# The low part of the rotary query over 128 rows of the key tile instead of 64

## The chip, the core and the metric

The kernel runs on one core of a Trainium2 chip. The metric is device time in microseconds (us), the median of several runs. The engines are called PE (TensorE, matmuls), PEld (the loading of PE's weights), DVE (VectorE), ACT (ScalarE), POOL (GpSimd) and SP (SyncE, which here only issues DMAs).

## The reference, cut to what matters

Two layers (DEPTH = 2) of a decoder trunk over 2048 tokens of width 1024, in float32. Each layer mixes gated linear attention (4 heads) with softmax attention (4 heads), and adds the projected result to the residual. The part that the change touches is the score of the softmax attention:

```python
q = concat([q[..., :128], apply_rope(q[..., 128:], cos, sin)])   # 128 plain + 64 rotary
k = concat([k[..., :128], apply_rope(k[..., 128:], cos, sin)])
for each block of 128 queries, each head:
    s = einsum('bhqd,bhkd->bhqk', q_blk, k) * 192 ** -0.5
    s = where(key <= query, s, -inf)
    p = softmax(s)
    o = einsum('bhqk,bhkd->bhqd', p, v)
```

A score is a dot product over 192 numbers: 128 plain ones and 64 rotary ones.

## The kernel before

**Precision.** Matmul operands are of type fp32r. To keep the precision of float32, each operand is split into a high part (the value rounded to fp32r) and a low part (the rest), and a product a·b is made as three: high·high, high·low and low·high.

**Stages.** Each layer has a first pass over 16 tiles of 128 tokens (input projection, linear attention), a second pass (gates, and the queries of all heads), then the softmax attention (`phase_b`), then the output projection (`phase_c`). `phase_b` goes through 32 steps, one for each head h (4) and each group g of 256 queries (8).

**Scores.** In a step, `scores` takes two blocks of 128 queries. For each it goes over the keys in banks of up to 512 columns, and makes each bank with five matmuls into one PSUM tile `sp`: three over the plain part (L951 to L953: query high · key high, query high · key low, query low · key high), then two over the rotary part. For the rotary part the tile `kr` holds the high part of the 64 rotary rows of the key in its rows 0 to 63 and the low part in its rows 64 to 127. The query's tile `qrr` holds the high part twice (`qrr[:, 0]`, rows 0 to 63 and 64 to 127), so that L954 makes high · high and high · low in one matmul over 128 rows. What is left, query low · key high, is L955, a matmul over 64 rows: `qrr[0:64, 1]` against `kr[0:64]`.

```python
T.matmul(o, lhsT=qrr[:, 0, ts_], rhs=kr[:, c0:c1], start=False, stop=False)            # L954
T.matmul(o, lhsT=qrr[0:64, 1, ts_], rhs=kr[0:64, c0:c1], start=False, stop=True)       # L955
```

DVE takes each bank out of PSUM (L959 with the mask on the diagonal, L962 elsewhere) and keeps the row maxima; ACT makes the exponentials (L969). There are two PSUM tiles `sp`.

**Values.** `values` of the step before runs interleaved with `scores` of the present one. For each 256 keys, PE transposes four 128x128 pieces of the probabilities into a tile `tp` (L88, of which there are three), ACT and DVE split it into the high part `ph` (L1004) and the low part `pl` (L1005), and PE multiplies with the values (L1024 to L1026). POOL scales the gates by the reciprocal of the softmax sum (L983, tile `gt`).

**Keys and queries.** `Gens` makes a step's keys, values and queries ahead of its scores: `lat` (loads), `kv` (projection; POOL writes the rotary key into `gst`, L869), `t` (transposes; ACT and DVE write the plain query `qn`, L886 and L887) and `tr` (rotary part; ACT and DVE write `kr` and `qrr`). A tile `q` holds `qn` and `qrr` of a step. There are four of them in `phase_b`; the queries of the first steps of a layer are made in the second pass, in tiles of their own.

**What sets the order.** On PE the order is that of the program, which interleaves scores, values and generation by estimated times (PACE, `pump`). On ACT, DVE, POOL and the DMA queues a scheduler sets it at build time. Every engine runs its instructions in its fixed order and waits for semaphores.

Of the kernel before, what the change touches and what calls it, by code (L numbers as in the profile page):

```python
# [9 lines left out]
F32 = mybir.dt.float32  # L10
# [9 lines left out]
P = 128  # L20
# [12 lines left out]
NSTG = 3  # L33
# pair of tiles and block of the second pass beside which a tile's queries are made; the pair that takes in the
# keys and values of each of the first head's first groups
QPOS = [(0, 3), (1, 1), (1, 3), (2, 1), (2, 3), (3, 0)] + [(p, b) for p in range(3, 7) for b in (1, 3)] + [(7, 0), (7, 1)]
PRE = (2, 4, 5, 6)
# pacing of phase B, per layer: lead of the generation of keys and queries over the attention (offset, ratio),
# lead of a step's scores over the step before's values (and in the last step), transposes ahead in the last step
PACE = [(-1.0, 0.151, 5.4, 2.1, 2, 10),  # L40
# [10 lines left out]
def trunk(ctx: ExitStack, tc: tile.TileContext, x, positions, norm_g, w_in, w_up, b_up, gla_g,  # L51
# [77 lines left out]

# [1 line left out]
    pos_f = cos.rearrange("p t c -> p (t c)")[0:NT, 0:P]  # L131

    def rotary(pool, ps):
        tr(ps[:, 0:NT], pos_f)
        pos = pool.tile([P, NT], F32, name="pos", bufs=1)
        V.tensor_copy(pos, ps[:, 0:NT])
        ang = pool.tile([P, NT, 32], F32, tag="osn", name="ang")
        V.tensor_tensor(out=ang, in0=pos.unsqueeze(2).broadcast_to([P, NT, 32]),
                        in1=cst[:, C_IF:C_IF + 32].unsqueeze(1).broadcast_to([P, NT, 32]), op=ALU.mult)
        kk = pool.tile([P, NT, 32], F32, tag="osn", name="kk")  # L140
        magic = 1.5 * 2.0 ** 23
        V.tensor_scalar(out=kk, in0=ang, scalar1=float(np.float32(1.0 / (2 * math.pi))), scalar2=magic,
                        op0=ALU.mult, op1=ALU.add)
        V.tensor_scalar(out=kk, in0=kk, scalar1=-magic, scalar2=None, op0=ALU.add)
        rest = 2 * math.pi
        for i in range(5):
            if i < 4:
                e = math.floor(math.log2(rest)) - 7
                c = math.floor(rest / 2.0 ** e) * 2.0 ** e
            else:  # L150
                c = float(np.float32(rest))
            V.scalar_tensor_tensor(out=ang, in0=kk, scalar=-c, in1=ang, op0=ALU.mult, op1=ALU.add)
            rest -= c
        lim = 3.1415925
        V.tensor_scalar(out=ang, in0=ang, scalar1=lim, scalar2=-lim, op0=ALU.min, op1=ALU.max)
        # cos(a) = sin(pi/2 - |a|)
        V.tensor_scalar(out=kk, in0=ang, scalar1=-1.0, scalar2=None, op0=ALU.mult)
        V.tensor_tensor(out=kk, in0=ang, in1=kk, op=ALU.max)
        V.tensor_scalar(out=kk, in0=kk, scalar1=-1.0, scalar2=math.pi / 2, op0=ALU.mult, op1=ALU.add)
        A.activation(out=cos, in_=kk, func=AF.Sin)  # L160
        tc.keep_in_program_order(A.activation(out=sin, in_=ang, func=AF.Sin))
        tc.keep_in_program_order(A.preload_act_table_set("natural_log_exp_and_others"))
        V.tensor_scalar(out=nsin, in0=sin, scalar1=-1.0, scalar2=None, op0=ALU.mult)

    def rope(eng, pool, o, i, n, c, s, ns, tag, u=None):
        # o, i: [P, n, 64]; c, s, ns: [P, n, 32]
        if u is None:
            u = pool.tile([P, n, 64], F32, tag=tag, name="ropeu", bufs=1)
        c2 = c.unsqueeze(2).broadcast_to([P, n, 2, 32])
        eng.tensor_tensor(out=u.rearrange("p n (a b) -> p n a b", a=2),  # L170
                          in0=i.rearrange("p n (a b) -> p n a b", a=2), in1=c2, op=ALU.mult)
        w = pool.tile([P, n, 64], F32, tag=tag + "w", name="ropew", bufs=1)
        eng.tensor_tensor(out=w[:, :, 0:32], in0=i[:, :, 32:64], in1=ns, op=ALU.mult)
        eng.tensor_tensor(out=w[:, :, 32:64], in0=i[:, :, 0:32], in1=s, op=ALU.mult)
        eng.tensor_tensor(out=o, in0=u, in1=w, op=ALU.add)

# [1 line left out]
    def layer_g8(l):  # L178
# [4 lines left out]
    def layer_small(l):  # L183
# [17 lines left out]
        sdma(r["gkr"], k_g[l, P:192].partition_broadcast(P))  # L201
        # against the high, low and high parts of the factor: high, high and low parts of the weights
        w3 = lp.tile([96, 256], F32, name="w3", bufs=1)
# [21 lines left out]

# [1 line left out]
    def wchunk(stage, kk, src, cols, n, name, scale, lo=None, us=None, halves=(0, 1)):  # L227
        """src: [1024, *] in DRAM, cols: (first here, first there, width); stage: gives a [P, >=kk, n] tile
        of which kk row blocks are filled at a time; scale: ("rows", g8) or ("gla", g)."""
        us, pieces = wpieces(stage, kk, src, cols, n, name, scale, lo, us, halves)  # L230
        for load, split in pieces:
            load()
            split()
        return us
# [53 lines left out]
    wi, wo = {}, {}  # L288
    # column groups of the input projection: c_q | c_kv | k_pe | the gate's low-rank factor; q | k; v; gates
    COLS = {"mi": ([(0, 1552, 448), (448, 1024, 16)], 464), "qk": ([(0, 0, 512)], 512),  # L290
# [16 lines left out]
    def boot_stage(which):  # L307
        # the first chunks are staged in units that nothing else uses yet
        got = {}

        def stage(half, k0):
            if half not in got:
                got[half] = unit([P, 4, COLS[which][1]], F32, f"boot{which}{half}")
            return got[half][:, k0:k0 + 2, :]

        return stage
# [24 lines left out]

    # ================= phase A, first pass: q, k, v, latents, rotary key; GLA =================
    def pass1(l, wp, pp, w1):
        sm = smalls[l]
        # the gate's low-rank factor as high | low | high parts (with a one for the bias), 32 columns each
        lr = w1.tile([P, 2, 3, 32], F32R, name="lr", bufs=1)
# [11 lines left out]
        def prep_r(t, n=2):  # L358
            # n tiles at a time
            if l == 0:  # L360
# [87 lines left out]
        def gla_b(t, qk):  # L448
# [6 lines left out]
            if t > 0:  # L455
# [8 lines left out]
                V.tensor_tensor(out=Tr[:, 1], in0=Tt, in1=Tr[:, 0].bitcast(F32), op=ALU.subtract)  # L464
            # high and low parts of the keys and (transposed, later) the queries
            kq = wp.tile([P, 4, 256], F32R, tag="stg", name="kq", bufs=3)
# [95 lines left out]
        def pair(p):  # L562
# [20 lines left out]
            if not more:  # L583
                # the second pass's weights, a piece at a time
                for which, blks in (("gt", (2, 3)), ("mg", (4, 5))):
# [24 lines left out]
        if l > 0:  # L610
            # stages that the end of the layer before takes in
            prep_x(0)
            yield
            prep_r(0, 1)
            yield
            prep_t(0, 0)
            yield
            prep_t(0, 1, True)
            yield
# [45 lines left out]

    # ================= phase A, second pass: output gates; keys and queries of the first head =================
    class pass2:
# [144 lines left out]

    # ================= keys, values and queries of 256 tokens of a head =================
    class Gens:
# [57 lines left out]
        def t(self, h, g):  # L872
# [5 lines left out]
            for i in range(2):  # L878
# [5 lines left out]
                                   in1=kn[:, 0, lt].bitcast(F32), op0=ALU.mult, op1=ALU.subtract)  # L884
            qn, qrr = self.aq(h, g)
            A.activation(out=qn[:, 0, :], in_=ps[:, 1, :], func=AF.Copy)  # L886
            V.tensor_tensor(out=qn[:, 1, :], in0=ps[:, 1, :], in1=qn[:, 0, :].bitcast(F32), op=ALU.subtract)  # L887
# [17 lines left out]

    # ================= phase B: attention, one head after the other =================
    def phase_b(l, pre):
        sm = smalls[l]
        goff, gratio, slead, slast, vlead, ypos = PACE[l]
        with tc.tile_pool(name=f"bp{l}", bufs=2, reuse_waits="tile") as bpl, \  # L910
# [15 lines left out]
            def scores(h, g):  # L926
# [6 lines left out]
                for i in range(2):  # L933
# [3 lines left out]
                    pt = both[:, i, :] if g < NG // 2 else unit([P, S], F32, f"p{l}")  # L937
                    # the last two of 512 + 128 keys become 320 + 320 where no boundary of a half lies between
                    edges = list(range(0, n, 512)) + [n]
# [5 lines left out]
                    for b in range(nbank):  # L945
# [8 lines left out]
                        T.matmul(o, lhsT=qrr[:, 0, ts_], rhs=kr[:, c0:c1], start=False, stop=False)  # L954
                        T.matmul(o, lhsT=qrr[0:64, 1, ts_], rhs=kr[0:64, c0:c1], start=False, stop=True)  # L955
                        w = c1 - c0
# [184 lines left out]

    # ================= phase C: output projection and residual =================
    def phase_c(l, wp, pp, yT01, ahead):
# [121 lines left out]
```

## Time and profile before

| | us |
|---|---|
| median of 3 runs | 2412.43 (2408.6 to 2414.42) |
| span of the profiled execution | 2413.8 |
| PE busy | 2364.2 (98% of the span) |
| PE weight loads (PEld) | 1938.4 (80%) |
| DVE busy | 1454.8 (60%) |
| ACT busy | 1315.5 (54%) |
| POOL busy | 411.8 (17%) |
| chain of work that ended last, PE's share | 90% |

The profiled execution's span is 1.4 us above the median; no other time of that execution is given, so the span stands for it. A matmul's row gives its start and its modelled duration. Matmuls are pipelined: the next one can start before the one before has ended, so that what a matmul costs in a dense stretch is read from the distance between starts, not from durations. The granted clock of PE in the profile is a mean between its two levels of 1.2 and 2.4 GHz, as a share of the higher.

### The profile page before, as it was taken

To read this page: it belongs to the slowest core of one execution; us is meant where nothing else is said; L and a number is where in the kernel's file an instruction comes from. 1 tells how busy PE (TensorE), PEld (TensorE's weight loads), DVE (VectorE), ACT (ScalarE), POOL (GpSimd) and SP (SyncE) were. 2 spreads that over 40 slices of the span, in tenths; PEclk is the share of its full clock that TensorE was granted. 3 is DMA by queue.
4 is the path that set the end of the run, shared out by engine and by line. 5 is a ranking of instruction groups with operands and counts; after the bars stand their busy time and mean duration, and the time that the engine had idled before them with its cause. 6 is when DMAs were issued, how large, how long until landed. Compare 5 with 4: busy or idle time off the path is not lost.

```text
span 2413.8 us, 37411 instructions
## 1 busy us (share of the span) xinstructions
PE 2364.2 (98%) x12821; PEld 1938.4 (80%) x12821; DVE 1454.8 (60%) x4376; ACT 1315.5 (54%) x3622; POOL 411.8 (17%) x593
## 2 busy tenths in 40 slices
PE   7999999999999999999999999999999999999999
PEld 5888888888787877788878888888887777777887
DVE  6676566666778777633365555656658777776222
ACT  6455456667766666532244444567666666665110
POOL 2111102333111112110011011033321111122000
PEclk9999999999999999999999999999999999999999
DMA  5111124432201111155531111344331111112542
GB/s 163 66 66 50 70 83 151 132 128 95 75 27 49 32 35 48 43 160 158 180 118 66 45 66 66 117 133 136 117 108 45 39 34 37 32 50 66 175 153 83
DMA packets 175859, 210.97 MB, mean 87 GB/s; under 512 B 17315, under 2 KB 128534, under 8 KB 175670
## 3 DMA queue, kind: packets, MB, share of 16 engines
q1 hardware_dynamic: 175254, 208.48, 26.8%
q8 instruction: 101, 1.65, 0.3%
q14 instruction: 88, 0.72, 0.1%
q0 software_dynamic: 416, 0.12, 0.1%
HBM read 128.86 MB, written 79.69 MB: 86 GB/s over the span
## 4 chain that ended last, share of the span: by engine, by line
PE 90%; ACT 4%; DVE 4%; DMA 1%; issue 1%; POOL 0%; SPq 0%; DVEq 0%; ACTq 0%
PE tp L88 10%; PE sp L955 5%; PE co L91 5%; PE co L92 5%; PE co L93 5%; PE sp L951 3%; PE o L1024 3%; PE o L1026 3%; PE sp L954 3%; PE sp L953 3%; PE sp L952 3%; PE o L1025 2%; PE gt L93 2%; PE gt L92 2%; PE gt L91 2%; PE mg L93 2%
## 5 line engine op out<-in xcount | busy, mean ns | idle before, releaser
L962 DVE TENSOR_SCALAR_CACHE_REDUCE p<-sp 128x512 f32<-128x512 f32 (+5 forms) x304 | 174.0, 575 | 61.0 <-PE sp L955 53.1
L383 POOL TENSOR_TENSOR hf<-hT 128x512 f32<-128x512 f32 x64 | 83.5, 1305 | 744.2 <-DVE hT L382 348.8
L1004 ACT ACTIVATE ph<-tp 128x512 fp32r<-128x512 f32 x224 | 130.8, 594 | 124.7 <-PE tp L88 111.9
L1005 DVE TENSOR_TENSOR pl<-tp,ph 128x512 fp32r<-128x512 f32 x224 | 152.6, 688 | 58.1 <-ACT ph L1004 56.2
L1024 PE MATMUL o<-ph,v 128*128 128x256 f32 x576 | 176.7, 307 | 3.1 <-ACT ph L1004 1.7
L1026 PE MATMUL o<-pl,v 128*128 128x256 f32 x576 | 176.7, 307 | 1.3 <-DVE pl L1005 0.9
L91 PE MATMUL co<-wo_h,yTs 128*128 128x512 f32 x448 | 174.5, 389 | 0.0
L93 PE MATMUL co<-wo_h,yTs 128*128 128x512 f32 x448 | 174.3, 389 | 0.0
L92 PE MATMUL co<-wo_l,yTs 128*128 128x512 f32 x448 | 174.3, 389 | 0.0
L969 ACT ACTIVATE p<-p,nm 128x128 f32<-128x128 f32 (+15 forms) x128 | 153.8, 1201 | 35.3 <-DVE nm L968 29.4
L88 PE MATMUL tp<-cst,p 128*128 128x128 f32 x1088 | 168.4, 276 | 0.3 <-DVE pl L1005 0.2
L1174 DVE TENSOR_TENSOR xo<-co,xo 128x512 f32<-128x512 f32 x64 | 44.2, 691 | 204.8 <-PE co L93 204.8
L1025 PE MATMUL o<-ph,v 128*128 128x256 f32 x576 | 161.3, 280 | 0.0
L1166 ACT ACTIVATE yTs<-yst 128x1024 fp32r<-128x1024 f32 x28 | 29.7, 1061 | 229.1 <-PE co L93 188.9
L951 PE MATMUL sp<-kn,q 128*128 128x512 f32 (+3 forms) x320 | 134.8, 421 | 8.7 <-ACT q L886 5.2
L955 PE MATMUL sp<-kr,q 64*128 64x512 f32 (+3 forms) x320 | 142.1, 454 | 0.0
L88 PEld LDWEIGHTS tp<-cst,p 128*128 128x128 f32 x1088 | 121.9, 141 | 13.7 <-issue 9.6
L983 POOL TENSOR_SCALAR gt<-gt,rl 128x128 f32<-128x128 f32 x128 | 77.4, 616 | 313.3 <-DVE rl L981 136.4
L1024 PEld LDWEIGHTS o<-ph,v 128*128 128x128 f32 x576 | 108.9, 189 | 24.0 <-issue 12.2
L955 PEld LDWEIGHTS sp<-kr,q 64*128 64x128 f32 x320 | 57.1, 183 | 86.1 <-issue 79.0
L869 POOL TENSOR_SCALAR gst<-kpe,rk 128x64 f32<-128x64 f32 x128 | 55.3, 447 | 402.7 <-PE tp L88 187.4
L1026 PEld LDWEIGHTS o<-pl,v 128*128 128x128 f32 x576 | 108.8, 189 | 17.7 <-issue 6.8
(285 smaller groups left out, 6995.6 us busy)
## 6 DMA issues: line engine op xcount, KB each, us to landing
hd<-hf SPq DMA_DIRECT2D x32, 512.0 KB, 2.8
hf<-hd SPq DMA_DIRECT2D x32, 512.0 KB, 3.8
stg<-in_w_in SPq DMA_DIRECT2D x28, 512.0 KB, 4.7
yst<-yd SPq DMA_DIRECT2D x28, 512.0 KB, 4.7
qd<-qs SPq DMA_DIRECT2D x32, 384.0 KB, 2.9
gst<-qd SPq DMA_DIRECT2D x64, 192.0 KB, 2.5
xt<-in_x SPq DMA_DIRECT2D x16, 512.0 KB, 3.4
od<-osn SPq DMA_DIRECT2D x32, 256.0 KB, 2.1
```

What stands on the lines that cost most here:

```text
L88: T.transpose(o, i, ident[:k, :k])
L91: T.matmul(o, lhsT=lh, rhs=rh, start=start, stop=False)
L92: T.matmul(o, lhsT=lh, rhs=rl, start=False, stop=False)
L93: T.matmul(o, lhsT=ll, rhs=rh, start=False, stop=stop)
L951: T.matmul(o, lhsT=qn[:, 0, ts_], rhs=kn[:, 0, k0:k1], start=True, stop=False)
L955: T.matmul(o, lhsT=qrr[0:64, 1, ts_], rhs=kr[0:64, c0:c1], start=False, stop=True)
L962: V.tensor_scalar(out=pt[:, c0:c0 + w], in0=sp[:, 0:w], scalar1=0.0, scalar2=-3e38, op0=ALU.add, op1=ALU.max, accum_out=mx[:, m:m + 1])
L969: A.activation(out=pt[:, 0:n], in_=pt[:, 0:n], func=AF.Exp, bias=nm, accum_out=rl[:, i:i + 1])
L1005: V.tensor_tensor(out=pl, in0=ps, in1=ph.bitcast(F32), op=ALU.subtract)
L1024: T.matmul(o[:, s], lhsT=vh, rhs=ph[:, j, s], start=(kb == 0), stop=False)
L1025: T.matmul(o[:, s], lhsT=vl, rhs=ph[:, j, s], start=False, stop=False)
L1026: T.matmul(o[:, s], lhsT=vh, rhs=pl[:, j, s], start=False, stop=(last and j == 1))
```

## The change

L955 now takes all 128 rows: `qrr[:, 1]` against `kr`. Rows 64 to 127 of `qrr[:, 1]` are new and hold zeros, so the product is the same. POOL writes these zeros, 64 partitions by 256 numbers, once for each step, when `t` takes the step's tile `q`. There are 64 such writes in the two layers. Some comments are removed and one line is added, so that lines behind L885 have a number that is one higher (L955 becomes L956).

```diff
             qn, qrr = self.aq(h, g)
+            G.memset(qrr[64:128, 1, :].bitcast(F32), 0.0)
             A.activation(out=qn[:, 0, :], in_=ps[:, 1, :], func=AF.Copy)
...
                         T.matmul(o, lhsT=qrr[:, 0, ts_], rhs=kr[:, c0:c1], start=False, stop=False)
-                        T.matmul(o, lhsT=qrr[0:64, 1, ts_], rhs=kr[0:64, c0:c1], start=False, stop=True)
+                        T.matmul(o, lhsT=qrr[:, 1, ts_], rhs=kr[:, c0:c1], start=False, stop=True)
```

On PE, in the first layer, at the second step of `phase_b` (its first bank of 320 keys, with a transpose of the step before ahead of it and behind it), the rows of the kernel before are:

```order
L88 MATMUL tp<-cst,p_6507 128x128 [waits Activation_49]
L951 MATMUL sp<-kn_4695,q_6399 128x320 [waits DVE_49,PE_49]
L952 MATMUL sp<-kn_4695,q_6399 128x320
L953 MATMUL sp<-kn_4695,q_6399 128x320
L954 MATMUL sp<-kr_4697,q_6399 128x320
L955 MATMUL sp<-kr_4697,q_6399 128x320
L88 MATMUL tp<-cst,p_6507 128x128 [waits Activation_49]
```

and those of the changed kernel are:

```order
L88 MATMUL tp<-cst,p_6511 128x128 [waits Activation_49]
L952 MATMUL sp<-kn_4695,q_6401 128x320 [waits DVE_49,PE_49]
L953 MATMUL sp<-kn_4695,q_6401 128x320
L954 MATMUL sp<-kn_4695,q_6401 128x320
L955 MATMUL sp<-kr_4697,q_6401 128x320
L956 MATMUL sp<-kr_4697,q_6401 128x320 [waits Pool_49]
L88 MATMUL tp<-cst,p_6511 128x128 [waits Activation_49]
```

Nothing moved on PE: in the whole program it has the same matmuls in the same order. The last of the five now waits for POOL, here and at the same place of the second layer; at no other place does PE's stream get a further wait, since waits that are already there cover the rest.

On POOL, in the middle of `phase_b` of the first layer, a piece of the difference (a `gst` row is the rotary key of a step, a `gt` row the gate of a step, `MEMSET q` the zeros):

```order
+L886 MEMSET q 64x256 [waits PE_49,Activation_49,Pool_49]
+L869 TENSOR_SCALAR gst<-kpe,rk 128x64 [waits DMAHW0_49,DVE_49,Pool_49]
+L869 TENSOR_SCALAR gst<-kpe,rk 128x64
+L984 TENSOR_SCALAR gt<-gt,rl 128x128 [waits DMAHW4_49,DVE_49]
+L984 TENSOR_SCALAR gt<-gt,rl 128x128 [waits DMAHW5_49,Activation_49]
+L886 MEMSET q 64x256 [waits PE_49,Pool_49]
+L869 TENSOR_SCALAR gst<-kpe,rk 128x64 [waits DVE_49,Pool_49]
+L869 TENSOR_SCALAR gst<-kpe,rk 128x64
```

The zeros of a step stand among the rotary keys and the gates of nearby steps. They wait until PE has read the tile `q` for the last time in the step four before, and a `gst` or a `gt` may stand behind them.

## Rows read from the trace of the kernel before

**Rows 1.** Head of the page: span; busy time, share, instructions by engine.

```profile
span 2413.8 us, 37411 instructions
PE 2364.2 (98%) x12821; PEld 1938.4 (80%) x12821; DVE 1454.8 (60%) x4376; ACT 1315.5 (54%) x3622; POOL 411.8 (17%) x593
```

**Rows 2.** Windows: length; busy PE, PEld, DVE, ACT, POOL; clock, DMA share, GB/s.

```profile
606.00:1020.00 414.00, 409.58 (x2471) 321.13 (x2469) 302.75 (x1082) 263.71 (x702) 70.01 (x125) 1.00 0.14 42
1802.00:2215.00 413.00, 408.44 (x2466) 319.76 (x2465) 301.99 (x1082) 262.32 (x701) 70.48 (x125) 1.00 0.14 41
```

**Rows 3.** One line's instructions: L955 on PE, durations min/median/max ns, first and last start.

```profile
L955 PE MATMUL sp<-kr,q x320: 306/492/502, 606.3 to 2215.3; 64*128 64x512 f32 x112, 64*128 64x128 f32 x16, 64*128 64x384 f32 x16, 64*128 64x320 f32 x16
```

**Rows 4.** Waits: engine, tile, line <- releaser: us in total, times, longest.

```profile
PE sp L951 <- ACT q L886: 5.2, 7, 1.0
...
PE sp L951 <- DVE p L962: 2.8, 2, 1.4
...
DVE p L962 <- PE sp L955: 53.1, 84, 2.9
```

**Rows 5.** Timeline of a bank of 512 keys: start, us, engine, line, operation [idle before].

```profile
1004.08 0.40 PE L952 MATMUL sp<-kn,q 128*128 128x512 f32 x1
1004.08 0.19 PEld L953 LDWEIGHTS sp<-kn,q 128*128 128x128 f32 x1
1004.31 0.40 PE L953 MATMUL sp<-kn,q 128*128 128x512 f32 x1
...
1004.54 0.39 PE L954 MATMUL sp<-kr,q 128*128 128x512 f32 x1
...
1004.87 0.18 PEld L955 LDWEIGHTS sp<-kr,q 64*128 64x128 f32 x1 [0.36 <-issue]
1004.87 0.49 PE L955 MATMUL sp<-kr,q 64*128 64x512 f32 x1
1005.29 0.19 PEld L1024 LDWEIGHTS o<-ph,v 128*128 128x128 f32 x1 [0.24 <-issue]
1005.29 0.39 PE L1024 MATMUL o<-ph,v 128*128 128x256 f32 x1
...
1005.51 0.28 PE L1025 MATMUL o<-ph,v 128*128 128x256 f32 x1
...
1005.63 0.28 PE L1026 MATMUL o<-pl,v 128*128 128x256 f32 x1
```

**Rows 6.** Timeline of PE at the end of a bank of 256 keys.

```profile
999.95 0.28 PE L954 MATMUL sp<-kr,q 128*128 128x256 f32 x1
1000.16 0.38 PE L955 MATMUL sp<-kr,q 64*128 64x256 f32 x1
1000.47 0.39 PE L1026 MATMUL o<-pl,v 128*128 128x256 f32 x1
1000.69 0.23 PE L1024 MATMUL o<-ph,v 128*128 128x128 f32 x1
```

**Rows 7.** Groups of PE by shape: busy us, mean ns | idle before.

```profile
L955 PE MATMUL sp<-kr,q 64*128 64x512 f32 x208 | 100.6, 490 | 0.0
...
L954 PE MATMUL sp<-kr,q 128*128 128x512 f32 x208 | 82.2, 397 | 0.0
```

**Rows 8.** Short windows inside the first attention stage (columns as in rows 2).

```profile
624.00:642.00 18.00, 17.68 (x121) 14.66 (x119) 15.40 (x59) 12.86 (x40) 4.67 (x10) 1.00 0.18 52
840.00:858.00 18.00, 18.00 (x96) 12.81 (x94) 14.65 (x58) 12.73 (x38) 2.90 (x6) 1.00 0.18 52
952.00:956.00 4.00, 2.64 (x13) 1.98 (x12) 3.08 (x10) 3.06 (x10) 0.54 (x1) 0.78 0.51 147
```

**Rows 9.** Groups of POOL: a tile of 128x256, and the constants of 128x1.

```profile
L714 POOL TENSOR_TENSOR ll<-lat,lh 128x256 fp32r<-128x256 f32 x32 | 27.5, 859 | 2.5
...
L1252 POOL MEMSET const-float32-0.0<- 128x1 f32 x1 | 0.1, 99 | 0.2 <-issue 0.2
```

**Rows 10.** Timeline of POOL: a gate that waited long.

```profile
1004.78 1.18 POOL L983 TENSOR_SCALAR gt<-gt,rl 128x128 f32<-128x128 f32 x2 [19.48 <-DVE rl L981]
```

## The prediction

> **What bounds the kernel now.** I read the head of the page first: PE is busy for 98% of the span, and the next engine, DVE, for 60% [rows 1]. A busy PE doesn't prove that PE does useful work, so I looked next at the two stages in which the changed line runs, 606 to 1020 us and 1802 to 2215 us. There PE is without an instruction for 414 - 409.6 = 4.4 us and 413 - 408.4 = 4.6 us; DVE is busy for 302.8 of 414 us (73%), ACT for 64% [rows 2]. The waits say the same: the largest of PE's scores are 5.2 us for ACT and 2.8 us for DVE, while DVE waited 53.1 us for the last matmul of a bank [rows 4]. So in these stages PE sets the pace, and a shorter PE stream shortens the kernel. L955 runs 320 times, all of them in these two stages [rows 3].
>
> Then I read one bank start by start, since the distance between two starts, not the duration, is what a matmul takes of PE's time. The reader should see three things [rows 5]. From L952 to L953 to L954, all of 128 rows, the starts are 0.23 us apart, and L953's weights are loaded while L952 runs. From L954 to L955 it is 0.33 us, and L955's weights start to load only when L955 itself starts, after 0.36 us of idle loader. From L955 to the next matmul (L1024) it is 0.42 us, again with a late load, and that next one needs 0.22 us until L1025, where L1025 to L1026, of the same width, need 0.12 us.
>
> **What the change removes.** The steady distance for 512 columns is 0.23 us. L955 costs 0.33 - 0.23 = 0.10 us ahead of it, 0.42 - 0.23 = 0.19 us behind it, and 0.22 - 0.12 = 0.10 us one matmul later: 0.39 us a bank [rows 5]. With 256 columns the same three distances are 0.21, 0.31 and 0.22 us, against 0.12 us: 0.09, 0.19 and 0.10 [rows 6]. So the surcharge doesn't depend on the width; it belongs to the border between a matmul of 128 rows and one of 64. In the program's order 71 of the 320 are followed by transposes. For these I count the first two parts and not the third, since the rows that I lean on show it only ahead of fp32r matmuls.
>
> Sum: 320 x (0.10 + 0.19) = 92.8 us, and 249 x 0.10 = 24.9 us, together 118 us. With the third part everywhere it would be 125 us, which I keep for the range. The matmul that stays should take what L954 takes, which has the same tiles' shapes over 128 rows: 397 ns in place of 490 by the group means [rows 7], and 0.23 us from start to start. The step taken here is that what makes L955 dear is its 64 rows, and that the row of L954 is the right one for it afterwards.
>
> **What the change adds.** POOL writes 64 blocks of zeros, 64 x 256 each. No such write is in the trace. The cheapest fill there takes 99 ns (one column), a two-operand pass over 256 columns takes 859 ns [rows 9]. I take the middle, an estimate of 0.45 us, since a fill reads nothing but has the larger one's width: 64 x 0.45 = 29 us, at most 55, of an engine that is idle for about 2000 us. It can't give time back, since it is work alone. On the path to the end it costs 0: a step's zeros are written when its tile q is made, and the code lets that run up to three steps ahead of the scores. What hides it is that lead; without it each fill would cost PE up to 0.86 us, 64 x 0.86 = 55 us. Two places where PE explicitly waits for POOL would cost 2 x 0.86 = 1.7 us if none of the fill were hidden; I take 0. Behind a waiting fill on POOL stand rotary keys and gates; the keys feed transposes of a later step, so they have the same lead. DMA and SP get nothing new; PE's order doesn't move.
>
> **Where the stall goes.** With 118 us gone, each stage has 414 - 59 = 355 us. DVE's 302.8 us are then 85% of it, ACT's 263.7 are 74%. DVE is late next. Two estimates from rows. First, waits grow with load: if they go as the busy share over the idle share, 0.73/0.27 = 2.7 becomes 0.85/0.15 = 5.7, and PE's 9 us of idle time become 19, so 10 us are lost. Second, where one head ends and the next begins DVE is dense: 15.40 and 14.65 of 18 us [rows 8], and 18 us shortened by 14% are 15.4. There DVE sets the pace for a while; eight such places at 0.5 us give 4 us. I take 14 us together, and for the range from 0 to 56 (below).
>
> **The sum.** 118 - 14 = 104 us. The profiled span is 2413.8 us, and the median is 1.4 us below it. 2413.8 - 104 = 2309.8 by the span, and 2308 us as a median.
>
> **Rivals.**
>
> *DVE takes the place of PE: 2350 us.* The values need `pl` from DVE for each 256 keys, 224 times in all, and the lead of the transposes is only one such piece. If each comes 0.25 us late after the change, 56 us of the 118 are lost: 2412 - 62 = 2350. For it: 85% load, a strict order on DVE, two banks in PSUM. The clock would add to it: around the one place where PE waits 1.4 us for DVE [rows 4], PE is busy for 2.64 of 4 us and the granted clock is 0.78, a mix of the levels 2.4 and 1.2 GHz [rows 8]. Against it: DVE waits 53.1 us for PE at the banks, and PE 2.8 us for DVE [rows 4].
>
> *The 64 rows are not what costs: 2412 us.* L955 is also the last of its five, the one that closes the bank and signals DVE. If that makes the surcharge, it stays, and the POOL work changes nothing. Against it: 0.10 us come ahead of L955, and the load of its weights is late, which a signal at its end can't cause [rows 5].
>
> The Trainium skill, "TensorE: Matmul & The Clock Gate" (Why this matters for your kernels), holds that a single matmul over 32 rows takes the same time as one over 128; by this rule alone padding changes nothing and the time stays at 2412 us. The trace agrees for a weight load (0.18 against 0.19 us) but not for the matmul (0.49 against 0.40 us, 0.33 and 0.42 against 0.23 us from start to start) [rows 5]. Another page of the Trainium skill, "TensorEngine Tiling (Array Packing)" (Key Properties), says that a change of the tiling mode drains the engine; by it the surcharge sits at the border and goes with it, as in the sum above.
>
> *The zeros come too late: slower, 2454 us.* A gate on POOL waited 19.48 us for DVE [rows 10]. If the zeros of the step that is about to run stood behind such a gate, the last matmul of its first bank would wait, and all of PE behind it. It decides from 118/64 = 1.8 us a step on; at 2.5 us a step it costs 160 us: 2412 - 118 + 160 = 2454. Against it: a tile q is made up to three steps ahead, and ACT's write into the same tile waits for the same release today without holding PE for more than 5.2 us in all [rows 4].
>
> **How the numbers follow.** Forecast 2308 us, chance 0.70. DVE in PE's place 0.19, no effect of the rows 0.06, zeros too late 0.05. The first two are faster, so faster by more than 0.3% (about what a measurement of this kernel can tell from no change) has 0.89, within 0.3% 0.06, slower 0.05. The low end is the full 125 us with no wait gained, 2412 - 125 = 2287, taken as 2286. The high end takes in the rival at 2350, taken as 2352. The other two rivals, 0.11, are left out.
>
> **What would show it.** The steps of the stage: L956 at 0.23 us from L955, the next matmul 0.23 us behind it, and L956's weights loaded while L955 runs; a mean duration near 397 ns for 512 columns. Each stage near 414 - 52 = 362 us, DVE near 84% of it. PE's waits for DVE and ACT some 20 us in all; far more, above all ahead of L1026 and L952, would be the first rival. Waits of PE for POOL near zero; fills of about 0.45 us. All stages outside the two unchanged. The prediction is wrong if L956 keeps its 0.33 and 0.42 us, or if PE's waits eat more than 50 us.

## The result, and the profile after

| | before | after |
|---|---|---|
| median | 2410.85 us | 2303.01 us |
| ratio | | 0.9551, 95% interval 0.9537 to 0.9566 |
| span of the profiled execution | 2413.8 us | 2302.5 us |

The change saves 107.8 us, or 4.5%. The forecast was 104 us and 2308 us. The head of the page of the changed kernel, which answers to [rows 1]:

```profile
span 2302.5 us, 37532 instructions
PE 2255.0 (98%) x12821; PEld 1948.1 (85%) x12821; DVE 1440.9 (63%) x4376; ACT 1311.4 (57%) x3622; POOL 431.1 (19%) x657
```

PE has as many instructions as before, and is 109 us less busy; POOL has 64 more, the zeros. The windows of the two attention stages answer to [rows 2] (length; then busy PE, PEld, DVE, ACT, POOL; clock, DMA share, GB/s):

```profile
605.00:963.50 358.50, 354.04 (x2464) 324.20 (x2463) 295.71 (x1082) 261.36 (x702) 77.34 (x152) 1.00 0.16 47
1745.50:2103.00 357.50, 353.76 (x2460) 324.01 (x2460) 294.20 (x1082) 259.52 (x700) 77.66 (x149) 1.00 0.16 47
```

Practically all of the gain is in these two. By the starts of the first and the last low rotary matmul of a stage, the first stage went from 413.9 us (606.3 to 1020.3) to 359.2 us (604.6 to 963.9), and the second from 412.9 to 358.2 us: 54.7 us each, 109.4 together. What lies between the stages went from 782.1 to 781.5 us, and what lies behind the second from 198.5 to 199.0. PE is without an instruction for 4.5 and 3.7 us of the stages; it was 4.4 and 4.6.

The timeline of the changed kernel at two banks of 512 keys answers to [rows 5] (start, us, engine, line; L956 is L955 of before):

```profile
949.37 0.39 PE L955 MATMUL sp<-kr,q 128*128 128x512 f32 x1
949.37 0.19 PEld L956 LDWEIGHTS sp<-kr,q 128*128 128x128 f32 x1
949.60 0.39 PE L956 MATMUL sp<-kr,q 128*128 128x512 f32 x1
...
949.83 0.39 PE L952 MATMUL sp<-kn,q 128*128 128x512 f32 x1
...
950.06 0.40 PE L953 MATMUL sp<-kn,q 128*128 128x512 f32 x1
```

From L955 to L956, on to L952 and on to L953 it is 0.23 us each time, and L956's weights are loaded while L955 runs. Before, the first two distances were 0.33 and 0.42 us [rows 5], and the load began only with the matmul. The third was 0.34 us where, as here, a matmul of 512 columns follows (608.83 to 609.17 in the kernel before, against the steady 0.23):

```profile
608.46 0.44 PE L955 MATMUL sp<-kr,q 64*128 64x384 f32 x1
608.83 0.50 PE L951 MATMUL sp<-kn,q 128*128 128x512 f32 x1
609.17 0.40 PE L952 MATMUL sp<-kn,q 128*128 128x512 f32 x1
```

Together that is 0.39 to 0.40 us at such a bank.

Groups and waits of the changed kernel: the fills on POOL (busy us, mean ns | idle before), and the longest waits that answer to [rows 4]:

```profile
L886 POOL MEMSET q<- 64x256 f32 x64 | 19.1, 307 | 127.2 <-PE sp L956 102.1 <-PE mg L93 20.9 <-PE gt L92 2.0
```

```profile
PE sp L952 <- ACT q L887: 5.0, 7, 1.0
...
PE sp L952 <- DVE p L963: 1.6, 3, 0.7
```

```profile
DVE p L963 <- PE sp L956: 18.1, 32, 2.5
```

A fill takes 0.31 us. POOL waited 102 us for PE to release the tile q; PE has no wait for POOL among its waits. Ahead of the scores, PE's waits for ACT and DVE did not grow (5.0 and 1.6 us, from 5.2 and 2.8). DVE's wait for a bank fell from 53.1 to 18.1 us: that part of its idle time was taken up.

### The profile page after: what moved, and what is told of

It reads as the page before. It is cut to its first block, busy times and chain, and to the rows that moved or that the text cites. A ratio compares the mean times of both kernels' runs of the same rounds, so it can differ in the third digit from the quotient of the medians.

```text
span 2302.5 us, 37532 instructions
## 1 busy us (share of the span) xinstructions
PE 2255.0 (98%) x12821; PEld 1948.1 (85%) x12821; DVE 1440.9 (63%) x4376; ACT 1311.4 (57%) x3622; POOL 431.1 (19%) x657
## 4 chain that ended last, share of the span: by engine, by line
PE 89%; ACT 4%; DVE 4%; DMA 2%; issue 1%; POOL 0%; SPq 0%; DVEq 0%; ACTq 0%
PE tp L88 10%; PE co L91 5%; PE co L92 5%; PE co L93 5%; PE sp L952 3%; PE sp L955 3%; PE sp L956 3%; PE sp L954 3%; PE sp L953 3%; PE o L1027 3%; PE gt L93 2%; PE gt L91 2%; PE gt L92 2%; PE o L1026 2%; PE o L1025 2%; PE mg L93 2%
## 5 line engine op out<-in xcount | busy, mean ns | idle before, releaser
L963 DVE TENSOR_SCALAR_CACHE_REDUCE p<-sp 128x512 f32<-128x512 f32 (+5 forms) x304 | 173.2, 573 | 22.9 <-PE sp L956 18.1
L1027 PE MATMUL o<-pl,v 128*128 128x256 f32 x576 | 170.6, 296 | 2.0 <-DVE pl L1006 1.5
L1025 PE MATMUL o<-ph,v 128*128 128x256 f32 x576 | 168.2, 292 | 3.3 <-ACT ph L1005 2.3
L1026 PE MATMUL o<-ph,v 128*128 128x256 f32 x576 | 161.4, 280 | 0.0
L952 PE MATMUL sp<-kn,q 128*128 128x512 f32 (+3 forms) x320 | 129.4, 404 | 7.3 <-ACT q L887 5.0
L954 PE MATMUL sp<-kn,q 128*128 128x512 f32 (+3 forms) x320 | 116.5, 370 | 0.0
L953 PE MATMUL sp<-kn,q 128*128 128x512 f32 (+3 forms) x320 | 116.3, 364 | 0.0
L955 PE MATMUL sp<-kr,q 128*128 128x512 f32 (+3 forms) x320 | 115.1, 366 | 0.4
```

The source lines that it names most:

```text
L952: T.matmul(o, lhsT=qn[:, 0, ts_], rhs=kn[:, 0, k0:k1], start=True, stop=False)
L953: T.matmul(o, lhsT=qn[:, 0, ts_], rhs=kn[:, 1, k0:k1], start=False, stop=False)
L954: T.matmul(o, lhsT=qn[:, 1, ts_], rhs=kn[:, 0, k0:k1], start=False, stop=False)
L963: V.tensor_scalar(out=pt[:, c0:c0 + w], in0=sp[:, 0:w], scalar1=0.0, scalar2=-3e38, op0=ALU.add, op1=ALU.max, accum_out=mx[:, m:m + 1])
L1025: T.matmul(o[:, s], lhsT=vh, rhs=ph[:, j, s], start=(kb == 0), stop=False)
L1026: T.matmul(o[:, s], lhsT=vl, rhs=ph[:, j, s], start=False, stop=False)
```

## What pays, the border or the matmul

All experiments below were run beside the kernel before, whose median was 2411 to 2412 us in each batch.

**Only the zeros.** The zeros are written, and the matmul stays at 64 rows.

```diff
+            G.memset(qrr[64:128, 1, :].bitcast(F32), 0.0)
```

> The kernel before with the zeros of the change written by POOL and never read; the matmul stays at 64 rows. Theory (the zeros are hidden): 2411 us, within 4 us, with 64 fills of 0.31 us on POOL. Rival (the fills hold up keys and gates behind them on POOL, and the gain of the change is that much larger on PE): 2411 plus up to 64 x 0.3 = 19 us, that is 2415 to 2430 us.

Measured: 2411.7 us, ratio 0.9997 (0.9987 to 1.0007). The zeros cost nothing that can be measured, and the time lies below the rival's 2415 to 2430 us: the rival falls.

**The 64-row matmul third of the five.** It no longer closes the bank.

```diff
                         T.matmul(o, lhsT=qn[:, 0, ts_], rhs=kn[:, 1, k0:k1], start=False, stop=False)
+                        T.matmul(o, lhsT=qrr[0:64, 1, ts_], rhs=kr[0:64, c0:c1], start=False, stop=False)
                         T.matmul(o, lhsT=qn[:, 1, ts_], rhs=kn[:, 0, k0:k1], start=False, stop=False)
-                        T.matmul(o, lhsT=qrr[:, 0, ts_], rhs=kr[:, c0:c1], start=False, stop=False)
-                        T.matmul(o, lhsT=qrr[0:64, 1, ts_], rhs=kr[0:64, c0:c1], start=False, stop=True)
+                        T.matmul(o, lhsT=qrr[:, 0, ts_], rhs=kr[:, c0:c1], start=False, stop=True)
```

> The kernel before with the 64-row matmul put third of the five of a bank, so that L954's counterpart over 128 rows closes the bank. Theory (the surcharge belongs to the borders between 64 and 128 rows): it moves with the matmul, 0.10 us ahead of it, 0.19 us behind it, 0.10 us one later, and the third part is now paid at all 320: 2411 + 71 x 0.10 = 2418 us, between 2408 and 2425. Rival (the surcharge belongs to the matmul that closes the bank and signals): the 64-row matmul costs the steady 0.23 us in its new place; if what closes the bank pays for that, the time stays at 2411 with the surcharge seen behind the 128-row matmul, and if the signal costs only with 64 rows, it falls to about 2303 us.

Measured: 2428.7 us, ratio 1.0066 (1.0048 to 1.0084). The timeline of PE at two banks (here L953 is the 64-row matmul and L955 closes the bank):

```profile
1006.13 0.40 PE L952 MATMUL sp<-kn,q 128*128 128x512 f32 x1
1006.46 0.49 PE L953 MATMUL sp<-kr,q 64*128 64x512 f32 x1
1006.88 0.50 PE L954 MATMUL sp<-kn,q 128*128 128x512 f32 x1
1007.22 0.40 PE L955 MATMUL sp<-kr,q 128*128 128x512 f32 x1
1007.46 0.40 PE L951 MATMUL sp<-kn,q 128*128 128x512 f32 x1
1007.69 0.39 PE L952 MATMUL sp<-kn,q 128*128 128x512 f32 x1
```

The three distances of 0.33, 0.42 and 0.34 us moved with the 64-row matmul, and the 128-row matmul that now closes the bank has the steady 0.24 us behind it. So the rival that puts the surcharge down to closing a bank falls. The time lies above the range of the forecast for this run (2408 to 2425 us), and the search for the reason showed what the prediction had miscounted. In the kernel before not all 64-row matmuls stand alone: the scheduler, which in `phase_b` also sets PE's order (ahead of the prediction this document says that the program does, which holds for the other stages), puts 20 of the 320 right behind another one, so that there are 300 runs of 64-row matmuls. One such place in the trace of the kernel before (two rows of one line are merged as x2):

```profile
634.50 0.71 PE L954 MATMUL sp<-kr,q 128*128 128x512 f32 x2
635.14 0.73 PE L955 MATMUL sp<-kr,q 64*128 64x512 f32 x2
635.81 0.66 PE L88 MATMUL tp<-cst,p 128*128 128x128 f32 x4
```

Two of them take 0.67 us up to the next matmul, where two alone would take 2 x 0.42 = 0.84. In this experiment there are 320 runs, all followed by an fp32r matmul: 20 x 0.39 + 71 x 0.10 = 15 us more than before, against 17 measured. The count explains the size, but not to the microsecond: PE's idle time in the two stages also grew, from 9.0 to 14.3 us, and its order differs in places.

**Two 64-row matmuls of half the columns.**

```diff
-                        T.matmul(o, lhsT=qrr[0:64, 1, ts_], rhs=kr[0:64, c0:c1], start=False, stop=True)
+                        ch = (c0 + c1) // 2
+                        T.matmul(sp[:, 0:ch - c0], lhsT=qrr[0:64, 1, ts_], rhs=kr[0:64, c0:ch], start=False, stop=False)
+                        T.matmul(sp[:, ch - c0:c1 - c0], lhsT=qrr[0:64, 1, ts_], rhs=kr[0:64, ch:c1], start=False, stop=True)
```

> The kernel before with the 64-row matmul of each bank cut into two 64-row matmuls of half the columns, one right behind the other. Theory (borders pay): one border in and one out as before, the two halves take together what the whole one took: 2411 us, within 8 us; from the first half to the second the start-to-start distance is that of a plain matmul of 256 columns, 0.12 us. Rival (each matmul over 64 rows pays its own surcharge): 320 more surcharges of 0.29 to 0.39 us, 2504 to 2536 us.

Measured: 2421.4 us, ratio 1.0036 (1.0023 to 1.0049): 10 us more, which is 2 us past the theory's bound of 8, and far from the rival's 93 to 125. The timeline of PE:

```profile
1004.94 0.40 PE L954 MATMUL sp<-kr,q 128*128 128x512 f32 x1
1005.27 0.38 PE L956 MATMUL sp<-kr,q 64*128 64x256 f32 x1
1005.49 0.27 PE L957 MATMUL sp<-kr,q 64*128 64x256 f32 x1
1005.70 0.45 PE L951 MATMUL sp<-kn,q 128*128 128x384 f32 x1
1005.99 0.34 PE L952 MATMUL sp<-kn,q 128*128 128x384 f32 x1
1006.16 0.34 PE L953 MATMUL sp<-kn,q 128*128 128x384 f32 x1
```

This splits the surcharge. The distances are 0.33, 0.22, 0.21 and 0.29 us, where 0.23, 0.12, 0.12 and 0.17 would be steady: 0.10 ahead of the border in, 0.10 behind the first matmul past it, 0.09 ahead of the border out, 0.12 behind the first matmul past that. A second 64-row matmul pays no border of its own. So each border costs about 0.2 us, half of it ahead of the first matmul past the border and half behind it, and the way in and out together 0.39 us. Of the 10 us, 8 more runs than before account for 3 us (in a few banks the scheduler put other matmuls between the halves). The starts in the trace show where the other 7 are: the two halves take longer than the whole took, the more so the narrower they are. At a bank of 512 columns they take 0.429 us up to the next matmul, where the whole took 0.422; at 128 columns 0.336 against 0.254. A steady stream has the same limit: over 128 rows, matmuls of 128 columns start 0.11 us apart, hardly less than those of 256 (0.12).

**96 rows instead of 128.**

```diff
-                        T.matmul(o, lhsT=qrr[:, 1, ts_], rhs=kr[:, c0:c1], start=False, stop=True)
+                        T.matmul(o, lhsT=qrr[0:96, 1, ts_], rhs=kr[0:96, c0:c1], start=False, stop=True)
```

> The changed kernel with the low part multiplied over 96 rows (zeros in rows 64 to 95) instead of 128. The projection of the gate's low-rank factor, L423, is a matmul over 96 rows in the trace of the kernel before, and its neighbours over 128 rows stand at steady distances (0.21, 0.13, 0.21 us). Theory (what pays is the border to a matmul of 64 rows, and 96 rows count as 128): 2303 us, within 5 us. Rival (any border between matmuls of different row counts pays): 2411 us.

Measured: 2305.1 us, ratio 0.9552 (0.9536 to 0.9568), the time of the changed kernel within the noise. The timeline of PE at a bank of 256 keys shows the steady 0.12 us throughout:

```profile
949.07 0.28 PE L955 MATMUL sp<-kr,q 128*128 128x256 f32 x1
949.19 0.28 PE L956 MATMUL sp<-kr,q 96*128 96x256 f32 x1
949.31 0.29 PE L1027 MATMUL o<-pl,v 128*128 128x256 f32 x1
949.43 0.22 PE L1025 MATMUL o<-ph,v 128*128 128x128 f32 x1
```

So not every difference in rows makes a border: 96 beside 128 doesn't, 64 beside 128 does.

## What sets the pace after the change

The prediction held that DVE is late next and put 14 us on it. Two runs of the changed kernel move DVE's load by about the same step, down and up.

**One pass of DVE to POOL**, and **the same pass twice on DVE** (one diff each):

```diff
-            V.tensor_tensor(out=kl, in0=lat[:, 2, tok], in1=kh.bitcast(F32), op=ALU.subtract)
+            G.tensor_tensor(out=kl, in0=lat[:, 2, tok], in1=kh.bitcast(F32), op=ALU.subtract)
```

```diff
             V.tensor_tensor(out=kl, in0=lat[:, 2, tok], in1=kh.bitcast(F32), op=ALU.subtract)
+            V.tensor_tensor(out=kl, in0=lat[:, 2, tok], in1=kh.bitcast(F32), op=ALU.subtract)
```

> The changed kernel once more, beside the next two: 2303 us, ratio to the kernel before 0.955.

> The changed kernel with one of DVE's passes in the attention stages (kl, the low part of the latents, 64 of 128x256 at 420 ns, 27 us in all) moved to POOL, where it takes about 0.86 us. It takes 13 us of 295 off DVE in each stage. Theory (after the change PE still sets the pace and DVE's share of 82% costs it almost nothing): 2303 us, between 2298 and 2306. Rival (DVE is by now a bound beside PE): a good part of the 27 us comes back, 2283 to 2293 us.

> The changed kernel with the same pass done twice on DVE: 13 us more in each stage, 308 of 358 us (86%), the share that DVE has where the low rotary matmul is left out. Theory (PE sets the pace): 2303 us, between 2300 and 2311. Rival (DVE is a bound beside PE): most of the 27 us is added, 2320 to 2330 us.

Measured, in one batch: the changed kernel 2303.3 us, ratio to before 0.9561 (0.9544 to 0.9578); with the pass on POOL 2308.3 us, 0.9581 (0.9562 to 0.9601); with the pass done twice 2307.0 us, 0.9572 (0.9557 to 0.9588). Windows of the first stage, the pass on POOL first, then the pass done twice:

```profile
605.00:965.00 360.00, 353.99 (x2462) 323.74 (x2461) 287.55 (x1044) 258.44 (x693) 97.42 (x177) 1.00 0.16 46
```

```profile
605.00:965.00 360.00, 355.47 (x2476) 325.89 (x2475) 303.15 (x1103) 259.02 (x696) 78.98 (x150) 1.00 0.16 47
```

DVE has 287.6 or 303.2 us to do in a stage that stays at 360 us; in the changed kernel of the same batch it has 296.8. The step is thus 9 and 6 us, not the expected 13. Taking load off brings nothing, so the rival falls. The 5 and 4 us by which the two are longer lie within the intervals, though the first time is 2 us above its theory's range too; with the pass on POOL, `kl` also takes 0.74 us in place of 0.42. As far as these two runs go, PE still sets the pace after the change. In both, the scheduler's order on PE differs in places from that of the changed kernel, which the comparison can't take out.

**Without the low rotary matmul.**

```diff
-                        T.matmul(o, lhsT=qrr[:, 0, ts_], rhs=kr[:, c0:c1], start=False, stop=False)
-                        T.matmul(o, lhsT=qrr[:, 1, ts_], rhs=kr[:, c0:c1], start=False, stop=True)
+                        T.matmul(o, lhsT=qrr[:, 0, ts_], rhs=kr[:, c0:c1], start=False, stop=True)
```

> The changed kernel without the low rotary matmul (query low times key high is left out of the scores; the zeros and the low part are still written). It takes 208 x 0.23 + 32 x (0.175 + 0.15 + 0.12) + 16 x 0.11 = 64 us of steady matmul time from PE and leaves DVE's work as it is. Theory (PE still sets the pace after the change, DVE costs only some us in waits): 2303 - 64 = 2239, with up to 15 us of added waits 2239 to 2254 us. Rival (after the change DVE sets the pace in the attention stages, at 295 of 358 us): less than half of the 64 us comes back, 2271 to 2303 us.

This kernel leaves a term of the scores out, so it is no better kernel. Measured: 2270.1 us, ratio 0.9411 (0.9396 to 0.9427). Of 64 us only 34 came back (the changed kernel of the same batch has 2303.8 us). That is between the two theories, 16 us above the one and 1 us below the other. Windows of both stages, and two of PE's waits:

```profile
607.00:945.00 338.00, 327.18 (x2305) 297.57 (x2304) 291.01 (x1082) 257.97 (x702) 76.26 (x151) 1.00 0.17 50
1730.00:2070.00 340.00, 327.13 (x2302) 297.43 (x2302) 291.67 (x1081) 257.79 (x700) 76.51 (x149) 1.00 0.17 49
```

```profile
PE o L1024 <- ACT ph L1004: 7.7, 9, 1.3
PE sp L952 <- ACT q L887: 7.6, 10, 1.6
```

PE's visible idle time grows from 4.5 and 3.7 us to 10.8 and 12.9, that is by 15 us. From the first score matmul of a stage to the last, the two stages are 39 us shorter (359.6 to 338.9 and 358.7 to 340.6), so 25 of the 64 are lost in them: the 15 of idle time, and 10 as starts further apart. The rest is lost outside them. DVE's share is 86%, much as with the pass done twice (303.2 of 360 is 84%), which cost 4 us. So a busy DVE alone hardly explains it. PE's waits point at the way from the transposes by ACT to the values and at ACT's queries. The scheduler's order on PE also changed in this kernel, more than in the two above. Which of the two took the 30 us stays open. What can be said is that here the next 64 us taken from PE gave back half, where this change's 109 came back whole.

## The same edit at the other matmuls over 64 rows

The linear attention's scores (L492) are the only other matmuls over 64 rows. They stand in groups of four a tile, alternating between the upper and the lower 64 rows, with much the same distances around them. In this kernel the query is written into a tile `qz` with zeros in the other half.

```diff
-                    rows = slice(r * 64, r * 64 + 64)
-                    T.matmul(ats[r][:, p, :], lhsT=qkT[rows, 2 + p, :], rhs=qkT[rows, p, :],
+                    T.matmul(ats[r][:, p, :], lhsT=qkT[:, p, :], rhs=qz[:, r, p, :],
...
+            A.activation(out=qz[0:64, 0], in_=ps[0:64, 0:2, :], func=AF.Copy)
+            V.tensor_copy(qz[64:128, 1], ps[64:128, 0:2, :])
```

> The changed kernel once more, beside the next two: 2303 us, ratio to the kernel before 0.955.

> The changed kernel, with the linear attention's score matmuls (L492, fp32, 64 rows, four a tile, in alternate halves of the rows) also over 128 rows: the query is written into a tile with zeros in the other half, on ACT and DVE. In the trace of the kernel before these stand with 0.32 us ahead of them where 0.23 is steady, and the matmul behind them needs 0.34 us where 0.23 is steady. Theory (borders pay in the same way here): 32 groups, 0.39 us each, 12 us less, 2291 us, if the four matmuls take as long over 128 rows as over 64. Rival (two 64-row matmuls in different halves run at the same time, and 128 rows lose that): the group of eight passes takes about 0.85 us in place of 0.46, which gives the 0.39 back: 2303 us, or a little more from the added work on ACT and DVE.

Measured, in one batch: the changed kernel 2303.8 us, ratio 0.955 (0.9536 to 0.9565); with 128 rows in the linear attention 2310.4 us, 0.9582 (0.9569 to 0.9595): 6.6 us slower, and far from the theory's 2291. Timeline of PE at one group, in the changed kernel and then in this one (x8 merges the passes of four fp32 matmuls):

```profile
63.95 0.40 PE L93 MATMUL vp<-wv_h,hT 128*128 128x512 f32 x1
64.28 0.71 PE L492 MATMUL at<-qkT 64*128 64x128 f32 x8
64.93 0.50 PE L91 MATMUL vp<-wv_h,hT 128*128 128x512 f32 x1
65.27 0.40 PE L92 MATMUL vp<-wv_l,hT 128*128 128x512 f32 x1
```

```profile
109.11 0.40 PE L93 MATMUL vp<-wv_h,hT 128*128 128x512 f32 x1
109.35 1.05 PE L495 MATMUL at<-qz,qkT 128*128 128x128 f32 x8
110.16 0.47 PE L91 MATMUL vp<-wv_h,hT 128*128 128x512 f32 x1
110.47 0.39 PE L92 MATMUL vp<-wv_l,hT 128*128 128x512 f32 x1
```

With 64 rows the way through the group is 0.33 + 0.65 + 0.34 = 1.32 us, with 128 rows 0.24 + 0.81 + 0.31 = 1.36 us. The starts of the single passes, which these rows merge, show both sides. Over 64 rows the passes start in pairs, 0.007 us apart, and from the start of one pair to that of the next it is 0.11 us; the two passes of the last pair signal separately, so they are of two matmuls, one in each half of the rows. Over 128 rows it is 0.11 us from pass to pass. So eight passes take eight steps in place of four, 0.44 us more. Both borders are gone in return: 0.24 us ahead in place of 0.33; a first step of 0.11 in place of 0.21; and from the last pass over the next matmul to the one after it 0.03 + 0.31 = 0.34 us, as in a steady stream (0.11 + 0.23), in place of 0.20 + 0.34. That gives the expected 0.39 us back. The rival was right, in its mechanism too: in different halves two 64-row matmuls run at the same time. The 0.05 us or so that are left make under 2 us in 32 groups; five of the groups also stand longer inside, 2.5 us together, in part at waits for DVE's copy into `qz` (1.1 us of PE's and its loader's idle time). The rest of the 6.6 us is not pinned to a row. None of the runs here that make the whole product beats the changed kernel.

## Why the prediction was right, step by step

**The price of a border was right.** 0.10, 0.19 and 0.10 us were read from [rows 5] and [rows 6] as a surcharge that doesn't depend on the width. The timeline after shows all three gone, and two experiments show them moving with the 64-row matmul and not growing with a second one. As PE has the same matmuls in the same order before and after, the two traces can be laid one on the other, distance by distance. Over the 300 runs the mean saving is 0.097 us on the way in, 0.176 on the way out, and one matmul later 0.099 where that is an fp32r matmul. Where a transpose follows (71 times) it is 0.055, which the sum put at 0.

**The count was too high.** The step that says that 320 matmuls pay 0.29 us and 249 of them 0.10 more took each matmul for a run of its own. By 300 runs, 71 of them followed by transposes, the term is 300 x 0.29 + 229 x 0.10 = 110 us in place of 118. The stages gave back 109.4. Laid one on the other, the traces give 29.0 us on the way in, 52.9 on the way out, 22.4 and 3.9 one matmul later, 0.8 inside the 20 pairs, and 1.1 at all other distances, 110 together.

**The loss to DVE was too high.** The prediction took 14 us: 10 for waits that grow with DVE's share, 4 for the dense places between heads. DVE's share did go to 295.7 of 358.5 us, 82%, near the 85% of the estimate. But PE's idle time stayed at 4.5 and 3.7 us, where the estimate had 19 together, and the distances that are no border's did not grow: the term came out at about nothing. So PE's waits did not go as DVE's busy share over its idle share here. The 4 us rest on a misreading besides: the two windows of [rows 8] that are said to stand where one head ends are in the middle of heads (by their first banks of 128 keys, heads begin at 606, 701, 810 and 919 us). After the change the same work takes 16.7 and 14.9 us, and PE is idle there for 0.3 and 0.0 us, though DVE is busy for 92% and 97% of it. The two errors, 8 us too much gained and about 14 too much lost, cancelled for the most part; the time of 2308 us came closer than its steps deserve, and that is luck.

**The zeros cost PE nothing, as said.** They took 307 ns against an estimate of 450, between the ends of 99 and 859 ns [rows 9]. Writing them alone left the time where it was, and the rival in which they come too late has no wait to show.

**Of the other rivals**, DVE in PE's place didn't come in, and closing the bank wasn't the cause. That the rows don't matter (2412 us) missed by 109 us. Among neighbours of their own kind 64 rows do take no longer than 128: where a half of 256 columns stands between other 64-row matmuls (20 places in the run with two halves), the next one starts 0.12 us behind it. What is dear is the change from one to the other. Why 64 rows make such a change and 96 don't, no run here shows.

## What to carry to other kernels

Read matmul costs from start to start, and look for the places where a shape change shows as a late weight load and a longer distance on both sides. A matmul over 64 rows among ones over 128 costs 0.39 us here besides its own time; fill it up to 128 (or 96) rows with zeros if a free engine can write them ahead. Several such matmuls side by side pay once, so that sorting them together may do as well; that was not tried. Leave groups alone that use both halves of the rows in turn, and count runs in the order that the scheduler made, not matmuls in the source.

## What had not been expected of the hardware

- 96 rows beside 128 rows cost no border: 0.12 us from start to start at 256 columns, and 2305.1 us for the whole kernel against 2303.
- A border is paid at two places: about 0.10 us ahead of the first matmul past it and about 0.10 us behind that one.
- Two fp32 matmuls of 64 rows in different halves start 0.007 us apart, and the pairs 0.11 us apart; over 128 rows it is 0.11 us from pass to pass.
